# Seven-product weight combinations: sums formed by accumulating transfers on GpSimd's queue instead of subtractions on VectorE

## The chip, the cores and the metric

The kernel runs on one core of one Trainium2 chip. The metric is device time in microseconds (us) of one execution, and the compared figure is the median of several executions. Five engines matter: TensorE (PE, with its weight loads PEld), VectorE (DVE), ScalarE (ACT), GpSimd (POOL) and SyncE (SP), which here only issues transfers. A row of a profile such as "L808 ACT CAST whi<-raw" reads: line 808 of the kernel, on ScalarE, writes tile `whi` from tile `raw`.

## What is computed

Two layers of a decoder trunk on 256 tokens of width 2048, in float32. Nearly all the work is large matrix products of the 256 tokens with weights that are read once from memory.

```python
def hybrid_layer(x, ...):
    h = rms_norm(x, g_mix_pre)
    proj = h @ w_in                       # 2048 x 11776: pool, conv, q, k, v, swish gate, 3 branch gates
    u_pool, u_conv, q, k, v, g_ret, gate_pre = split(proj)
    y_pool = pool_mixer(u_pool, ...) @ w_pool_proj
    y_conv = conv_module(u_conv, ...) @ w_conv_proj
    y_ret = retention(q, k, v, g_ret, ...) @ w_ret_proj
    gates = sigmoid(gate_pre.reshape(B, S, 3, D))
    merged = gates[:, :, 0] * y_pool + gates[:, :, 1] * y_conv + gates[:, :, 2] * y_ret
    x = x + rms_norm(merged @ w_out, g_mix_post)
    h = rms_norm(x, g_ffn_pre)
    a, b = split(h @ w_ffn_in, 2)         # 2048 x 11264
    x = x + rms_norm((silu(a) * b) @ w_ffn_out, g_ffn_post)   # 5632 x 2048
    return x
```

## The kernel before

**Chunks and loads.** Every product is cut into chunks of 512 output columns (`chunks`; a chunk holds the weight, its first row, its depth in blocks of 128 rows, its first column, the name of the left operand, the function that takes the result away, and what must be finished first). Tokens come in two halves of 128, h = 0 and h = 1. A weight comes in loads of two blocks, a tile `raw` of 128 x 2 x 512 float32 (512 KB), issued by SP from a pool of six (`RAWBUFS`). `load()` splits a `raw` in two: ScalarE writes the rounded part `whi` (line 808) and VectorE the rest `wlo` (line 809). Both come from pools of seven (`WBLOCKS`). A product of one block with one half is three matmuls in a PSUM bank (lines 830 to 832: high by high, low by high, high by low).

**Order.** `items` is the planned list of loads. `multiply(0)` walks it for the first half; `multiply(1)` follows four loads behind (`LAG = 8` blocks) for the second half. In all that follows, a **pass** is one load against one half: two blocks, six matmuls. Splits stand as far ahead in the program as the seven buffers let them.

**Seven products.** 44 pairs of neighbouring chunks n, n+1 (`mixed`) save one product in eight on four of their blocks (a quad): rows r, r+1 and rows r+2, r+3, columns of n and of n+1 give a 2 x 2 matrix of weight loads

- b11 (upper rows, chunk n), b12 (upper rows, chunk n+1), b21 (lower rows, chunk n), b22 (lower rows, chunk n+1),

and the two token halves by the two row pairs give a 2 x 2 matrix of left operands a11, a12, a21, a22. Seven products replace eight: four weight combinations t1 to t4 are formed from the b blocks, and sums of the a blocks are formed once per left operand by `token_sums` (lines 187 to 206). Each of the seven is used in one pass only, since a combination belongs to both halves. The other loads of a pair, called P (chunk n) and Q (chunk n+1) below, take two passes each: six of each where the chunk is 16 blocks deep (40 pairs), four of each where it is 12 deep (the 4 pairs of the first part of the second feed-forward product).

The combinations are made in place on the `raw` tiles by VectorE:

```python
        if kind == "t1":
            kept["b12"] = fetch(i, n + 1, k)
            dve.tensor_tensor(kept["b11"], kept["b12"], kept["b11"], op=ALU.subtract)   # line 788
...
        elif kind == "t4":
            dve.tensor_tensor(kept["b21"], kept["b21"], kept["b22"], op=ALU.subtract)   # line 795
...
        if kind == "b22":                                                    # after its own split
            dve.tensor_tensor(kept["b12"], raw, kept["b12"], op=ALU.subtract)           # line 812
            dve.tensor_tensor(raw, raw, kept["b11"], op=ALU.subtract)                   # line 813
```

so a pair of depth 16 runs as P P P P P b11 t1 P b21 b22 Q t2 Q t3 Q t4 Q Q Q. Partial results of the seven are joined by four VectorE operations per pair (lines 868 to 882).

Of the kernel before, what the change touches and what calls it, by code (L numbers as in the profile page):

```python
# [18 lines left out]
P = 128  # L19
# [18 lines left out]
LAG = 8  # L38
WBLOCKS = 7
SLOTS = 24  # L40

# [36 lines left out]
def trunk(ctx: ExitStack, tc: tile.TileContext, x, x_cols, positions, g_mix_post, g_ffn_post, w_in, pool_w,  # L78
# [103 lines left out]
    def pre_norm_quad(h, c, gain, mixed):  # L182
        st["xT", h].append(split(transpose4(x_block(h, c)), gain[:, 4 * c:4 * c + 4]))
        if mixed and c == 3 and h == 1:
            add_sums("sum", "xT", 3)

    def token_sums(lhs, c):

        ts = [st[lhs, h][c] for h in range(2)]
        u = slot([P, 2, 4, P])  # L190
        for h in range(2):
            dve.tensor_tensor(u[:, h], ts[h][:, 0].bitcast(F32), ts[h][:, 1].bitcast(F32), op=ALU.add)
            yield 0.7
        a11, a12, a21, a22 = (u[:, h, 2 * i:2 * i + 2] for h in range(2) for i in range(2))
        s = slot([P, 4, 2, P])
        dve.tensor_tensor(s[:, 0], a21, a22, op=ALU.add)
        dve.tensor_tensor(s[:, 1], s[:, 0], a11, op=ALU.subtract)
        yield 0.9
        dve.tensor_tensor(s[:, 2], a11, a21, op=ALU.subtract)
        dve.tensor_tensor(s[:, 3], a12, s[:, 1], op=ALU.subtract)  # L200
        yield 0.9
        hi, lo = slot([P, 4, 2, P], F32R), slot([P, 4, 2, P], F32R)
        act.copy(hi, s)
        dve.tensor_tensor(lo, s, hi.bitcast(F32), op=ALU.subtract)
        st["S", lhs, c] = (hi, lo)
        yield 1.2
# [112 lines left out]
    def add_job(key, gen, light=False):  # L319
        jobs.append([key, gen, 0, light])  # L320

    def add_sums(key, lhs, c):
        jobs.insert(0, [(key, 0), token_sums(lhs, c), 0, True])

    def step_job(job):
        cost = next(job[1], None)
# [173 lines left out]
    def ev_rot(key, qd):  # L500
        def f(h, ps):
            if h == 0:
                st[key, qd] = slot([P, 4, SEQ])
            if key == "qT" and qd == 0:
                finish({("trig", 0)})
                tr = sm.tile([P, 3, 64], F32, name=nm("tr"), tag="tr", bufs=2)
                r = st["rstd", h]
                dve.tensor_scalar(tr[:, 0, :], trig["cos"][:, h * 64:(h + 1) * 64], r, None, op0=ALU.mult)
                dve.tensor_scalar(tr[:, 1, :], trig["sin"][:, h * 64:(h + 1) * 64], r, None, op0=ALU.mult)
                dve.tensor_scalar(tr[:, 2, :], tr[:, 1, :], -1.0, None, op0=ALU.mult)  # L510
                st["tr", h] = tr
# [12 lines left out]
            dve.tensor_tensor(a, a, b, op=ALU.add)  # L524
            dst = st[key, qd][:, :, h * P:(h + 1) * P]
            defer(2 * D_T, lambda: act.copy(dst, transpose4(a)))
            if key == "kT" and qd == 1 and h == 1:
                add_sums("sum", "xT", 3)
        return f

    def ev_v(qd):
# [26 lines left out]
    def ev_y(b, c):  # L558
        def f(h, ps):
# [10 lines left out]
            if b == 2:  # L570
# [3 lines left out]
                def put():  # L574
                    st["mT", h].append(split(transpose4(m)))
                    if h == 1 and c == 0:
                        add_sums("sum", "mT", 0)

                defer(2 * D_T, put)
        return f  # L580
# [38 lines left out]
    def ev_b(first):  # L619
        def f(h, ps, t=None):  # L620
# [9 lines left out]
            def put():  # L630
                hid.append(split(transpose4(u)))
                if first and h == 1:
                    add_sums("sum", "hid", 0)

            defer(D_T, put)
        return f
# [35 lines left out]
    for l in range(DEPTH):  # L672
        wi = w_in[l]

        def gate(b, c, needs=()):
            add(wi, 0, 16, Q_GATE + b * D + c * NB, "xT", ev_gate(b, c), needs)

        def project(b, c):
            w, name = ((w_pool_proj, "pool"), (w_conv_proj, "conv"), (w_ret_proj, "ret"))[b]
# [10 lines left out]
        for b in range(3):  # L690
            for c in (0, 2):
                mix(*GATE_QUADS[b])
                for cc in (c, c + 1):
                    gate(b, cc, ("sum", "sum2")[:len(GATE_QUADS[b])])
                for cc in (c, c + 1):
                    project(b, cc)
        for c in range(4):
            if c == 0:
                mix(0)
            add(w_out[l], 0, 16, c * NB, "mT", ev_out(l, c), ("sum",))  # L700
        ends.append(len(chunks))
        parts = ((0, 3), (3, 7), (7, 11))
        for p, (b0, b1) in enumerate(parts):
            last = p == len(parts) - 1
            for j in range(b0, b1):
                if j:
                    mix(3)
                add(w_ffn_in[l], 0, 16, j * NB, "xT", ev_a, ("sum",) if j else ())
                add(w_ffn_in[l], 0, 16, HIDDEN + j * NB, "xT", ev_b(j == b0))
            for c in range(4):  # L710
                if c == 0 or c == 2 and not last:
                    mix(0)
                add(w_ffn_out[l], b0 * 4, (b1 - b0) * 4, c * NB, "hid", ev_ffn(l, c, p, last), ("sum",))
        ends.append(len(chunks))

    SEVEN = (("b11", 0), ("t1", 0), ("b21", 2), ("b22", 2), ("t2", 0), ("t3", 0), ("t4", 2))


    paired = {0} | {e for e in ends[:-1]}
# [8 lines left out]
    while n < len(chunks):  # L728
        ks = list(range(0, chunks[n][2], LOAD))
        if n in mixed:  # L730
            ks = [k for k in ks if k // 4 not in mixed[n]]

            head = max(LAG // LOAD, len(ks) - 1) if len(mixed[n]) == 1 else len(ks)
            for k in ks[:head]:
                plan("", n, k)
            for q in mixed[n][:-1]:
                for kind, d in SEVEN:
                    plan(kind, n, 4 * q + d)
            q = 4 * mixed[n][-1]
            plan("b11", n, q)  # L740
            plan("t1", n, q)
            for k in ks[head:]:
                plan("", n, k)
            plan("b21", n, q + 2)
            plan("b22", n, q + 2)
            for k, kind, kq in zip(ks, ("t2", "t3", "t4"), (q, q, q + 2)):
                plan("", n + 1, k)
                plan(kind, n, kq)
            for k in ks[3:]:
                plan("", n + 1, k)  # L750
            side = (n, n + 1)
        else:
            side = (n, n + 1) if n in paired else (n,)
# [4 lines left out]
            final[m] = ks[-1] + LOAD - 1  # L758
        n += len(side)
        count[n] = len(items)  # L760
    raws = {}
    wt = {}
    banks = {}
    loaded = [0]
    done = [0, 0]

    def fetch(i, n=None, k=None):
        if n is None:
            n, k = items[i][1:]
        w, r0, kt, c0 = chunks[n][:4]  # L770
        r = (r0 + k) * P
        raw = wpool.tile([P, LOAD, NB], F32, name=nm("raw"), tag="raw", bufs=RAWBUFS)
        step = LOAD if i else 1
        for kk in range(0, LOAD, step):
            nc.sync.dma_start(raw[:, kk:kk + step], w[r + kk * P:r + (kk + step) * P, c0:c0 + NB]
                              .rearrange("(k p) n -> p k n", p=P))
        raws[i] = raw
        return raw

# [2 lines left out]
    def load():  # L782

        i = loaded[0]
        kind, n, k = items[i]
        if kind == "t1":
            kept["b12"] = fetch(i, n + 1, k)
            dve.tensor_tensor(kept["b11"], kept["b12"], kept["b11"], op=ALU.subtract)  # L788
            raw = kept["b11"]
        elif kind == "t2":  # L790
            raw = kept["b22"]
        elif kind == "t3":
            raw = kept["b12"]
        elif kind == "t4":
            dve.tensor_tensor(kept["b21"], kept["b21"], kept["b22"], op=ALU.subtract)  # L795
            raw = kept["b21"]
        elif kind == "b22":
            raw = kept[kind] = fetch(i, n + 1, k)
        else:
            if i not in raws:  # L800
                fetch(i)
            raw = raws.pop(i)
            kept[kind] = raw
        hi = wpool.tile([P, LOAD, NB], F32R, name=nm("whi"), tag="whi", bufs=WBLOCKS)
        lo = wpool.tile([P, LOAD, NB], F32R, name=nm("wlo"), tag="wlo", bufs=WBLOCKS)
        step = LOAD if i else 1
        for kk in range(0, LOAD, step):
            act.copy(hi[:, kk:kk + step], raw[:, kk:kk + step])  # L808
            dve.tensor_tensor(lo[:, kk:kk + step], raw[:, kk:kk + step], hi[:, kk:kk + step].bitcast(F32),  # L809
                              op=ALU.subtract)  # L810
        if kind == "b22":
            dve.tensor_tensor(kept["b12"], raw, kept["b12"], op=ALU.subtract)  # L812
            dve.tensor_tensor(raw, raw, kept["b11"], op=ALU.subtract)  # L813
        for kk in range(LOAD):
            wt[i + kk] = (hi[:, kk, :], lo[:, kk, :])
        loaded[0] += LOAD
# [18 lines left out]
    def mixed_product(kind, n, k, w):  # L835

        kk, last = k % 2, k % 2 == 1 and k // 4 == mixed[n][-1]
        lhs, outs = chunks[n][4], (chunks[n][5], chunks[n + 1][5])

        def a_part(h):  # L840
# [20 lines left out]
            bank(s_part(0))  # L861
        elif kind == "b22":
            product((0, n + 1), "mm0", s_part(3), w, False)
        elif kind == "t2":
            x = bank(s_part(1))
            if last:
                s = st["sum", 1, n]
                dve.tensor_tensor(s, s, x, op=ALU.add)
                st["sum", 0, n] = t2("dt", 2)
                dve.tensor_tensor(st["sum", 0, n], s, banks["t1", n], op=ALU.add)  # L870
        elif kind == "t3":
            x = bank(s_part(2))
            if last:
                s = st["sum", 1, n]
                dve.tensor_tensor(s, s, x, op=ALU.add)
        elif kind == "t4":
            y = product((1, n), "mm1", a_part(1), w, last)
            if last:
                assert items[done[1]][1:] > (n, final[n])
                s = st["sum", 1, n]  # L880
                outs[0](1, y, s)
                dve.tensor_tensor(s, s, banks["t1", n], op=ALU.add)

    def multiply(h):
        i = done[h]
# [4 lines left out]
                mixed_product(kind, n, k, wt.pop(i))  # L890
        else:
            w, r0, kt, c0, lhs, evac, needs = chunks[n]
            if k == (4 if mixed.get(n, mixed.get(n - 1)) == (0,) else 0):
# [158 lines left out]
```

## Time and profile before

| | |
|---|---|
| three runs, us | 2845.32, 2845.46, 2847.76 (median 2845.46) |
| profiled execution, us | 2846.71, its span on the core 2844.9 |
| TensorE busy | 2825.8 us, 12788 instructions, granted clock 0.999 |
| VectorE busy | 2257.6 us (79%) |
| ScalarE busy | 1434.2 us (50%) |
| GpSimd busy | 104.4 us (4%), no transfers on its queue |
| transfers | 569.78 MB, mean 200 GB/s |

A busy share says how long an engine held an instruction; the chain of waits says which engine ended last at each step. Matmuls overlap: one lasts 0.39 us in the records while a new one starts every 0.23 us, so the time of a matmul is read from the distance of two starts.

### The profile page before, as it was taken

How to read it: one execution, taken by the hardware profiler on the slowest of the kernel's cores; microseconds unless marked ns; L12 is line 12 of the kernel's file. 1: busy time of each engine (PE TensorE's matmuls, PEld its weight loads, DVE VectorE, ACT ScalarE, POOL GpSimd, SP SyncE). 2: the span in 40 equal slices, each digit the busy share in tenths (PEclk: the TensorE clock that was granted, in tenths of full speed). 3: DMA queues.
4: the chain of work that ended last, by engine and by line, in shares of the span. 5: the costliest groups of instructions: out<-in, count | busy, mean ns of one | idle time of the engine just before them, and what ended most of it. 6: DMA issues, size and time to landing. Idle time of an engine off the chain costs nothing.

```text
span 2844.9 us, 34694 instructions
## 1 busy us (share of the span) xinstructions
PE 2825.8 (99%) x12788; PEld 2333.2 (82%) x12788; DVE 2257.6 (79%) x2671; ACT 1434.2 (50%) x1638; POOL 104.4 (4%) x102
## 2 busy tenths in 40 slices
PE   9999999999999999999999999999999999999998
PEld 7888888888888888888888888888888888888887
DVE  6987888776888887787769778787768888887886
ACT  5444544554555554454554455455555554544553
POOL 0000001100100000000000000010000000000000
PEclk9999999999999999999999999999999999999999
DMA  8665655557655665665766655655676565656654
GB/s 306 189 191 172 202 183 188 178 191 259 187 199 200 215 199 172 220 198 192 243 213 186 191 175 177 208 178 180 207 263 189 185 215 188 218 174 201 217 194 166
DMA packets 293898, 569.78 MB, mean 200 GB/s; under 512 B 18272, under 2 KB 21600, under 8 KB 293728
## 3 DMA queue, kind: packets, MB, share of 16 engines
q1 hardware_dynamic: 293728, 567.57, 61.8%
q8 instruction: 100, 1.64, 0.2%
q14 instruction: 70, 0.57, 0.1%
HBM read 559.11 MB, written 8.39 MB: 199 GB/s over the span
## 4 chain that ended last, share of the span: by engine, by line
PE 96%; DVE 3%; ACT 0%; POOL 0%; issue 0%; DMA 0%; SPq 0%; DVEq 0%; POOLq 0%; ACTq 0%
PE mm L832 31%; PE mm L831 31%; PE mm L830 31%; PE tp L143 2%; DVE wlo L809 1%; ACT whi L808 0%; DVE slot L245 0%; PE tp L444 0%; DVE slot L137 0%; DMA raw<-in_w_in 0%; DVE ta L134 0%; DVE ta L464 0%; PE sc L408 0%; PE sc L452 0%; PE sc L434 0%
## 5 line engine op out<-in xcount | busy, mean ns | idle before, releaser
L808 ACT CAST whi<-raw 128x1024 fp32r<-128x1024 f32 (+1 forms) x1157 | 1200.7, 1052 | 1188.3 <-PE mm L831 842.7
L809 DVE TENSOR_TENSOR wlo<-raw,whi 128x1024 fp32r<-128x1024 f32 (+1 forms) x1157 | 1407.7, 1235 | 408.1 <-ACT whi L808 393.1
L830 PE MATMUL mm<-whi,slot 128*128 128x512 f32 x4008 | 1570.4, 392 | 1.2 <-ACT whi L808 0.7
L832 PE MATMUL mm<-wlo,slot 128*128 128x512 f32 x4008 | 1562.5, 390 | 3.6 <-DVE wlo L809 3.5
L831 PE MATMUL mm<-whi,slot 128*128 128x512 f32 x4008 | 1561.4, 390 | 0.7 <-DVE slot L137 0.6
L832 PEld LDWEIGHTS mm<-wlo,slot 128*128 128x128 f32 x4008 | 752.3, 188 | 164.0 <-DVE wlo L809 7.7
L830 PEld LDWEIGHTS mm<-whi,slot 128*128 128x128 f32 x4008 | 752.6, 188 | 155.5 <-ACT whi L808 3.7
L831 PEld LDWEIGHTS mm<-whi,slot 128*128 128x128 f32 x4008 | 752.9, 188 | 154.8 <-DVE slot L137 2.7
L365 DVE SCALAR_TENSOR_TENSOR slot<-slot,par,slot 128x237 f32<-128x237 f32 (+25 forms) x240 | 98.1, 461 | 0.5
L137 DVE TENSOR_TENSOR slot<-tp,slot 128x512 fp32r<-128x512 f32 x60 | 40.8, 685 | 47.4 <-ACT slot L136 47.4
L136 ACT CAST slot<-tp 128x512 fp32r<-128x512 f32 x60 | 35.2, 586 | 84.3 <-PE tp L143 84.3
L569 POOL TENSOR_TENSOR slot<-slot,tb 128x512 f32<-128x512 f32 x32 | 52.9, 1658 | 413.9 <-DVE tb L568 404.7
L237 POOL TENSOR_SCALAR ms_o<-ssq_t 128x1 f32<-128x1 f32 x8 | 1.5, 192 | 1472.8 <-DVE ssq_t L235 1472.8
L788 DVE TENSOR_TENSOR raw<-raw,raw 128x1024 f32<-128x1024 f32 x44 | 53.8, 1223 | 1.3
L813 DVE TENSOR_TENSOR raw<-raw,raw 128x1024 f32<-128x1024 f32 x44 | 53.7, 1221 | 0.9
L812 DVE TENSOR_TENSOR raw<-raw,raw 128x1024 f32<-128x1024 f32 x44 | 53.6, 1218 | 0.3
L795 DVE TENSOR_TENSOR raw<-raw,raw 128x1024 f32<-128x1024 f32 x44 | 53.6, 1218 | 0.2
L625 DVE TENSOR_TENSOR ta<-dt,mm 128x512 f32<-128x512 f32 x40 | 27.3, 683 | 21.5 <-PE mm L832 21.5
L143 PEld LDWEIGHTS tp<-ident,ta 128*128 128x128 f32 x272 | 33.8, 141 | 9.6 <-issue 1.1
L136 ACT CAST slot<-ta 128x512 fp32r<-128x512 f32 x40 | 24.8, 619 | 32.9 <-DVE ta L134 27.6
L143 PE MATMUL tp<-ident,ta 128*128 128x128 f32 x272 | 40.7, 272 | 0.3 <-DVE ta L379 0.2
L148 ACT ACTIVATE tb<-slot 128x512 f32<-128x512 f32 x48 | 30.0, 626 | 21.7 <-DVE slot L648 14.9
(136 smaller groups left out, 948.7 us busy)
## 6 DMA issues: line engine op xcount, KB each, us to landing
raw<-in_w_in SPq DMA_DIRECT2D x367, 512.0 KB, 4.0
raw<-in_w_ffn_in SPq DMA_DIRECT2D x352, 512.0 KB, 4.6
raw<-in_w_ffn_out SPq DMA_DIRECT2D x176, 512.0 KB, 4.7
raw<-in_w_out SPq DMA_DIRECT2D x64, 512.0 KB, 4.4
raw<-in_w_ret_proj SPq DMA_DIRECT2D x32, 512.0 KB, 5.5
raw<-in_w_pool_proj SPq DMA_DIRECT2D x16, 512.0 KB, 5.5
raw<-in_w_conv_proj SPq DMA_DIRECT2D x16, 512.0 KB, 5.7
x<-slot SPq DMA_DIRECT2D x12, 512.0 KB, 4.4
```

The source lines that it names most:

```text
L136: act.copy(t[:, 0], src)
L143: pe.transpose(tp[:, j, :], src[:, j * P:(j + 1) * P], ident)
L365: dve.scalar_tensor_tensor(acc[:, ct, s:], hT[:, ct, :SEQ - s], w[:, TAPS - 1 - s:TAPS - s], acc[:, ct, s:], op0=ALU.mult, op1=ALU.add)
L788: dve.tensor_tensor(kept["b11"], kept["b12"], kept["b11"], op=ALU.subtract)
L795: dve.tensor_tensor(kept["b21"], kept["b21"], kept["b22"], op=ALU.subtract)
L808: act.copy(hi[:, kk:kk + step], raw[:, kk:kk + step])
L809: dve.tensor_tensor(lo[:, kk:kk + step], raw[:, kk:kk + step], hi[:, kk:kk + step].bitcast(F32), op=ALU.subtract)
L812: dve.tensor_tensor(kept["b12"], raw, kept["b12"], op=ALU.subtract)
L813: dve.tensor_tensor(raw, raw, kept["b11"], op=ALU.subtract)
L830: pe.matmul(ps, a[0], w[0], start=first, stop=False)
L831: pe.matmul(ps, a[1], w[0], start=False, stop=False)
L832: pe.matmul(ps, a[0], w[1], start=False, stop=stop)
```

## The change

The signs in the seven products are chosen anew, so that every combination of weights is a sum:

- t1 = b11 + b12, t2 = t1 + b22, t4 = t2 + b21, all in the tile that b11 was loaded to; t3 = b22 + b12, in the tile of b22.

Each step is a transfer issued on GpSimd's queue that reads the other block from memory again and adds it to the tile (`accum_op=ALU.add`), after the tile's earlier content has been split. VectorE's four subtractions per pair are gone; the separate load of b12 is gone; four accumulating transfers per pair are new. The order of the loads becomes P P P P b11 P b22 P t1 b21 t3 Q t2 Q Q t4 Q Q Q (depth 16) and P P P P b11 b22 t1 b21 t3 Q t2 Q Q t4 Q (depth 12). The wait for the token sums moves to the pass of b22.

```diff
@@ token_sums
-        dve.tensor_tensor(s[:, 0], a21, a22, op=ALU.add)
+        dve.tensor_tensor(s[:, 0], a21, a22, op=ALU.subtract)
...
-        dve.tensor_tensor(s[:, 3], a12, s[:, 1], op=ALU.subtract)
+        dve.tensor_tensor(s[:, 3], a12, s[:, 1], op=ALU.add)
@@ planning of a mixed pair
+            head = LAG // LOAD + 1 - len(quads)
             for k in ks[:head]:
                 plan("", n, k)
...
+            seven("b11")
+            for k in ks[head:-1]:
                 plan("", n, k)
...
+            seven("b22")
+            for k in ks[max(head, len(ks) - 1):]:
+                plan("", n, k)
+            seven("t1", "b21", "t3")
+            for i, k in enumerate(ks):
                 plan("", n + 1, k)
...
+                if i == 0:
+                    seven("t2")
+                if i == min(2, len(ks) - 1):
+                    seven("t4")
@@ load()
+    ADDED = {"b11": (1, 0), "t1": (1, 2), "t2": (0, 2), "b22": (1, 0)}
...
-        if kind == "t1":
-            kept["b12"] = fetch(i, n + 1, k)
-            dve.tensor_tensor(kept["b11"], kept["b12"], kept["b11"], op=ALU.subtract)
...
+        if kind in ("t1", "t2", "t3", "t4"):
+            raw = kept[{"t3": "b22"}.get(kind, "b11"), k // 4]
...
-        if kind == "b22":
-            dve.tensor_tensor(kept["b12"], raw, kept["b12"], op=ALU.subtract)
-            dve.tensor_tensor(raw, raw, kept["b11"], op=ALU.subtract)
+        if kind in ADDED:
+            right, down = ADDED[kind]
+            gp.dma_start(raw, block(n + right, k - k % 4 + down), accum_op=ALU.add)
@@ mixed_product
+        if kind == "b22" and not kk:
+            finish({("sum", chunks[n][4], k // 4)})
...
         elif kind == "t2":
             x = bank(s_part(1))
             if last:
                 s = st["sum", 1, n]
                 dve.tensor_tensor(s, s, x, op=ALU.add)
                 st["sum", 0, n] = t2("dt", 2)
-                dve.tensor_tensor(st["sum", 0, n], s, banks["t1", n], op=ALU.add)
+                dve.tensor_tensor(st["sum", 0, n], banks["t1", n], s, op=ALU.subtract)
+                dve.tensor_tensor(s, s, banks["t3", n], op=ALU.add)
```

How the instructions stand, in one pair of the first layer's first feed-forward product (depth 16). ScalarE before; its rows are the splits in their order: b22 from its own `raw`, a Q, t2 (again from b22's tile `raw_1413`), a Q, t3 (from `raw_1398`, where b12 was), a Q, a SiLU for the preceding result, t4 (from b21's tile), a Q.

```order
L808 CAST whi_1414_6813<-raw_1413_6811 128x1024
L808 CAST whi_1417_6833<-raw_1416_6831 128x1024
L808 CAST whi_1421_6853<-raw_1413_6811 128x1024
L808 CAST whi_1424_6859<-raw_1423_6857 128x1024
L808 CAST whi_1426_6863<-raw_1398_6743 128x1024
L808 CAST whi_1432_6898<-raw_1431_6896 128x1024
L616 ACTIVATE sg_1420_6848<-ta_1419_6846,rstd_1241_5996 128x512
L808 CAST whi_1434_6903<-raw_1409_6792 128x1024
L808 CAST whi_1437_6909<-raw_1436_6907 128x1024
```

ScalarE of the changed kernel at the same place: t1 (tile `raw_1383`, that of b11), a transposed block, b21, t3 (tile `raw_1390`, that of b22), a Q, t2 (`raw_1383`), two Q, the SiLU, t4 (`raw_1383`), a Q.

```order
L810 CAST whi_1401_6777<-raw_1383_6688 128x1024
L137 CAST slot_1400_6768<-tp_1399_6763 128x512
L810 CAST whi_1405_6797<-raw_1404_6795 128x1024
L810 CAST whi_1407_6813<-raw_1390_6728 128x1024
L810 CAST whi_1410_6819<-raw_1409_6817 128x1024
L810 CAST whi_1415_6846<-raw_1383_6688 128x1024
L810 CAST whi_1418_6853<-raw_1417_6851 128x1024
L810 CAST whi_1422_6878<-raw_1421_6876 128x1024
L617 ACTIVATE sg_1414_6841<-ta_1413_6839,rstd_1234_5982 128x512
L810 CAST whi_1424_6882<-raw_1383_6688 128x1024
L810 CAST whi_1427_6888<-raw_1426_6886 128x1024
```

Three splits of one tile now follow each other here, with four instructions of ScalarE between the first and the second of them and three between the second and the third; t3 has moved ahead of t2.

GpSimd's queue of the changed kernel, from the end of the norm before the first feed-forward product to the second pair of it (before, the next instruction after these two norms' rows on this queue stood at the end of the layer).

```order
L126 TENSOR_SCALAR rstd_a_1258_6075<-ssq_t_1257_6073 128x1
L128 TENSOR_TENSOR rstd_1259_6077<-rstd_a_1258_6075,nhalf_78 128x1
L816 DMA raw_1305_6334<-in_w_ffn_in 128x2x512
L816 DMA raw_1313_6375<-in_w_ffn_in 128x2x512
L816 DMA raw_1305_6334<-in_w_ffn_in 128x2x512 x2
L816 DMA raw_1383_6688<-in_w_ffn_in 128x2x512
L816 DMA raw_1390_6728<-in_w_ffn_in 128x2x512
L816 DMA raw_1383_6688<-in_w_ffn_in 128x2x512 x2
```

For each pair the queue holds, in this order, the step to t1, the step to t3, the step to t2 and the step to t4, each behind the split of what the tile held.

More of the change, by code (lines that the diff above doesn't have):

```diff
@@ L184, in pre_norm_quad @@
         if mixed and c == 3 and h == 1:
-            add_sums("sum", "xT", 3)
+            add_sums("xT", 3)
     def token_sums(lhs, c):
@@ L320, in add_job, with add_sums @@
         jobs.append([key, gen, 0, light])
-    def add_sums(key, lhs, c):
-        jobs.insert(0, [(key, 0), token_sums(lhs, c), 0, True])
+    def add_sums(lhs, c):
+        jobs.insert(0, [("sum", lhs, c), token_sums(lhs, c), 0, True])
     def step_job(job):
@@ L527, in f @@
             if key == "kT" and qd == 1 and h == 1:
-                add_sums("sum", "xT", 3)
+                add_sums("xT", 3)
         return f
@@ L576, in put @@
                     if h == 1 and c == 0:
-                        add_sums("sum", "mT", 0)
+                        add_sums("mT", 0)
                 defer(2 * D_T, put)
@@ L632, in put @@
                 if first and h == 1:
-                    add_sums("sum", "hid", 0)
+                    add_sums("hid", 0)
             defer(D_T, put)
@@ L673, in trunk, with gate @@
         wi = w_in[l]
-        def gate(b, c, needs=()):
-            add(wi, 0, 16, Q_GATE + b * D + c * NB, "xT", ev_gate(b, c), needs)
+        def gate(b, c):
+            add(wi, 0, 16, Q_GATE + b * D + c * NB, "xT", ev_gate(b, c))
         def project(b, c):
@@ L693, in trunk @@
                 for cc in (c, c + 1):
-                    gate(b, cc, ("sum", "sum2")[:len(GATE_QUADS[b])])
+                    gate(b, cc)
                 for cc in (c, c + 1):
@@ L699, in trunk @@
                 mix(0)
-            add(w_out[l], 0, 16, c * NB, "mT", ev_out(l, c), ("sum",))
+            add(w_out[l], 0, 16, c * NB, "mT", ev_out(l, c))
         ends.append(len(chunks))
@@ L707, in trunk @@
                     mix(3)
-                add(w_ffn_in[l], 0, 16, j * NB, "xT", ev_a, ("sum",) if j else ())
+                add(w_ffn_in[l], 0, 16, j * NB, "xT", ev_a)
                 add(w_ffn_in[l], 0, 16, HIDDEN + j * NB, "xT", ev_b(j == b0))
@@ L712, in trunk @@
                     mix(0)
-                add(w_ffn_out[l], b0 * 4, (b1 - b0) * 4, c * NB, "hid", ev_ffn(l, c, p, last), ("sum",))
+                add(w_ffn_out[l], b0 * 4, (b1 - b0) * 4, c * NB, "hid", ev_ffn(l, c, p, last))
         ends.append(len(chunks))
-    SEVEN = (("b11", 0), ("t1", 0), ("b21", 2), ("b22", 2), ("t2", 0), ("t3", 0), ("t4", 2))
+    ADDED = {"b11": (1, 0), "t1": (1, 2), "t2": (0, 2), "b22": (1, 0)}
     paired = {0} | {e for e in ends[:-1]}
@@ L730, in trunk, with seven @@
         if n in mixed:
-            ks = [k for k in ks if k // 4 not in mixed[n]]
-            head = max(LAG // LOAD, len(ks) - 1) if len(mixed[n]) == 1 else len(ks)
+            quads = mixed[n]
+            ks = [k for k in ks if k // 4 not in quads]
+            def seven(*kinds):
+                for kind in kinds:
+                    for q in quads:
+                        plan(kind, n, 4 * q + (2 if kind in ("b21", "b22", "t4") else 0))
+            head = LAG // LOAD + 1 - len(quads)
             for k in ks[:head]:
                 plan("", n, k)
[L736 to L742, printed above, removed]
-                plan("", n, k)
-            plan("b21", n, q + 2)
-            plan("b22", n, q + 2)
-            for k, kind, kq in zip(ks, ("t2", "t3", "t4"), (q, q, q + 2)):
+            seven("b11")
+            for k in ks[head:-1]:
+                plan("", n, k)
+            seven("b22")
[3 more added lines that the diff above has]
+            for i, k in enumerate(ks):
                 plan("", n + 1, k)
-                plan(kind, n, kq)
-            for k in ks[3:]:
-                plan("", n + 1, k)
+                if i == 0:
+                    seven("t2")
+                if i == min(2, len(ks) - 1):
+                    seven("t4")
             side = (n, n + 1)
@@ L760, in trunk @@
         count[n] = len(items)
+    first = {}
+    for i, (kind, n, k) in enumerate(items):
+        if not kind:
+            first.setdefault(n, i)
     raws = {}
@@ L765, in trunk, with block, fetch @@
     done = [0, 0]
-    def fetch(i, n=None, k=None):
-        if n is None:
-            n, k = items[i][1:]
+    def block(n, k, kk=0, count=LOAD):
         w, r0, kt, c0 = chunks[n][:4]
-        r = (r0 + k) * P
+        r = (r0 + k + kk) * P
+        return w[r:r + count * P, c0:c0 + NB].rearrange("(k p) n -> p k n", p=P)
+    def fetch(i):
+        kind, n, k = items[i]
+        n += kind == "b22"
         raw = wpool.tile([P, LOAD, NB], F32, name=nm("raw"), tag="raw", bufs=RAWBUFS)
@@ L774, in fetch @@
         for kk in range(0, LOAD, step):
-            nc.sync.dma_start(raw[:, kk:kk + step], w[r + kk * P:r + (kk + step) * P, c0:c0 + NB]
-                              .rearrange("(k p) n -> p k n", p=P))
+            nc.sync.dma_start(raw[:, kk:kk + step], block(n, k, kk, step))
         raws[i] = raw
@@ L785, in load @@
         kind, n, k = items[i]
-        if kind == "t1":
-            kept["b12"] = fetch(i, n + 1, k)
[L788 to L798, printed above, removed]
+        if kind in ("t1", "t2", "t3", "t4"):
+            raw = kept[{"t3": "b22"}.get(kind, "b11"), k // 4]
         else:
@@ L802, in load @@
             raw = raws.pop(i)
-            kept[kind] = raw
+            kept[kind, k // 4] = raw
         hi = wpool.tile([P, LOAD, NB], F32R, name=nm("whi"), tag="whi", bufs=WBLOCKS)
@@ L863, in mixed_product @@
             product((0, n + 1), "mm0", s_part(3), w, False)
+        elif kind == "t3":
+            bank(s_part(2))
         elif kind == "t2":
@@ L869, in mixed_product @@
                 st["sum", 0, n] = t2("dt", 2)
-                dve.tensor_tensor(st["sum", 0, n], s, banks["t1", n], op=ALU.add)
[L871 to L875, printed above, removed]
+                dve.tensor_tensor(st["sum", 0, n], banks["t1", n], s, op=ALU.subtract)
+                dve.tensor_tensor(s, s, banks["t3", n], op=ALU.add)
         elif kind == "t4":
@@ L881, in mixed_product @@
                 outs[0](1, y, s)
-                dve.tensor_tensor(s, s, banks["t1", n], op=ALU.add)
+                dve.tensor_tensor(s, banks["t1", n], s, op=ALU.subtract)
     def multiply(h):
@@ L892, in multiply @@
             w, r0, kt, c0, lhs, evac, needs = chunks[n]
-            if k == (4 if mixed.get(n, mixed.get(n - 1)) == (0,) else 0):
+            if i == first[n]:
                 finish({(s, q) for s in needs for q in (0, h)})
```

## Prediction

> **What bounds the kernel now.** I read the busy times and the clock first, then the chain that ended last, then TensorE's waits, then single stretches.
>
> ```profile
> span 2844.9 us, 34694 instructions
> PE 2825.8 (99%) x12788; PEld 2333.2 (82%) x12788; DVE 2257.6 (79%) x2671; ACT 1434.2 (50%) x1638; POOL 104.4 (4%) x102
> PEclk9999999999999999999999999999999999999999
> PE 96%; DVE 3%; ACT 0%; POOL 0%; issue 0%; DMA 0%; SPq 0%; DVEq 0%; POOLq 0%; ACTq 0%
> ```
>
> TensorE is idle for 2844.9 - 2825.8 = 19.1 us, its clock is full, and 96% of the chain is its own. Two starts in an unbroken run give the price of a matmul:
>
> ```profile
> 1002.53 0.39 PE L830 MATMUL mm<-whi,slot 128*128 128x512 f32 x1
> ...
> 1011.38 0.39 PE L830 MATMUL mm<-whi,slot 128*128 128x512 f32 x1
> ```
>
> They are 39 matmuls apart: 8.85 / 39 = 0.227 us, so a pass (six) takes 1.36 us. The change neither removes nor adds a matmul. So what it can win lies inside the 19.1 us, while any new wait of TensorE adds to the time in full. Where the idle time lies, by stretches (columns: stretch, its length, TensorE busy and records, clock, transfers):
>
> ```profile
> 0.00:25.00 25.00, 22.26 (x82) 1.00 0.94 324
> 325.00:400.00 75.00, 72.41 (x357) 1.00 0.55 173
> 550.00:575.00 25.00, 24.09 (x113) 1.00 0.33 98
> 1400.00:1450.00 50.00, 48.29 (x225) 1.00 0.71 220
> 1700.00:1775.00 75.00, 74.31 (x365) 1.00 0.55 176
> 1975.00:2000.00 25.00, 24.08 (x109) 1.00 0.39 115
> 2825.00:2845.00 20.00, 11.14 (x50) 0.85 0.29 105
> ```
>
> The first and the last (2.7 and 8.9 us) are the start and the end of the program, which the change does not touch. Between them lie 2.6 + 0.9 + 1.7 + 0.7 + 0.9 = 6.8 us: about the most that can be won.
>
> **What goes.** VectorE's four subtractions per pair:
>
> ```profile
> L788 DVE TENSOR_TENSOR raw<-raw,raw 128x1024 f32<-128x1024 f32 x44 | 53.8, 1223 | 1.3
> L813 DVE TENSOR_TENSOR raw<-raw,raw 128x1024 f32<-128x1024 f32 x44 | 53.7, 1221 | 0.9
> L812 DVE TENSOR_TENSOR raw<-raw,raw 128x1024 f32<-128x1024 f32 x44 | 53.6, 1218 | 0.3
> L795 DVE TENSOR_TENSOR raw<-raw,raw 128x1024 f32<-128x1024 f32 x44 | 53.6, 1218 | 0.2
> PE mm L832 <- DVE wlo L809: 1.8, 2, 0.9
> ```
>
> That is 214.7 us of an engine that is beside the path nearly everywhere. The last row (TensorE's waits after 400 us) shows the two places where these subtractions do delay it: 0.9 us each, in the stretches at 550 and 1975, where `wlo` comes late because the subtractions and the token sums stand ahead of it. Those 1.8 us go. In the stretches 325 to 400 and 1700 to 1775, where retention shares VectorE with the first pair (3.3 us together), I count half, 1.6; the 1.7 us at 1400 lie at a norm and stay. Gain: 3.4 us, between 0 and 6.8. The four joining operations (L868 to L882) stay four on VectorE. SP loses 44 of its loads. The token sums keep their operations.
>
> **What comes: a round trip between two splits of one tile.** Before, a combination was ready 1.22 us after its inputs. Now t1, t2 and t4 each need: the split of what the tile holds, GpSimd's issue, the transfer, the next split. TensorE needs them in program order, so each has a fixed number of passes to hide in. ScalarE's splits are held by the seven buffers, not by the loads:
>
> ```profile
> ACT whi L808 <- PE mm L831: 842.7, 608, 4.4
> 1003.97 1.05 ACT L808 CAST whi<-raw 128x1024 fp32r<-128x1024 f32 x1
> 1005.05 1.22 DVE L809 TENSOR_TENSOR wlo<-raw,whi 128x1024 fp32r<-128x1024 f32 x1 [0.20 <-ACT whi L808]
> ```
>
> A split thus starts when the load seven places earlier has had its last pass, and takes 1005.05 + 1.22 - 1003.97 = 2.30 us to the end of `wlo`.
>
> Take the pair of depth 16. t2 stands seven places behind the fifth P; its split can start when that P's second-half pass ends, which runs interleaved with the pass of b21. From there to the pass of t4, TensorE has: t3 (one pass), the first Q with the sixth P's second half (two), t2, Q, Q: six passes, 8.16 us. Into that must go the split of t2 (2.30), the round trip L, and the split of t4 (2.30, less 0.45 since `wlo` is first read by the third matmul), with 0.1 for the signals. That leaves L = 8.16 - 2.30 - 1.85 - 0.1 = 3.9 us. **If the accumulating transfer takes longer than 3.9 us from the end of `wlo` to its landing, TensorE stands still for the rest, once per pair.** Behind the late split of t4 on ScalarE's queue wait the splits of the last three Q; each needs TensorE later, so they shift with it and cost nothing of their own. GpSimd's own waits cost nothing in the feed-forward stages, where its queue has no other work.
>
> The other round trips have more room: b11 to t1 eight passes less a split, 10.9 - 2.4 = 8.5 us; t1 to t2 seven passes, 9.5 - 2.4 = 7.1 us; b22 to t3 as b11. In the four pairs of depth 12 the room between t2 and t4 is five passes: 6.8 - 4.25 = 2.5 us. There b11, b22 and t1 stand side by side, and the three round trips from b11 to t4 follow each other in seventeen passes, 23.1 us: with four splits, 9.2 - 0.45, they leave 14.3 us, so that the wait is the larger of L - 2.5 and 3 L - 14.3.
>
> **The size of L.** No row of before has a transfer on GpSimd's queue. The nearest are the plain loads of the same 512 KB (first row: all feed-forward loads, median to landing; second: all loads into `raw`, least, median and most, 800 to 2000 us):
>
> ```profile
> raw<-in_w_ffn_in SPq DMA_DIRECT2D x352, 512.0 KB, 4.6
> DMA to landing us min/median/max: 3.4/4.5/7.1
> q1 hardware_dynamic: 293728, 567.57, 61.8%
> L125 POOL TENSOR_SCALAR rstd_a<-ssq_t 128x1 f32<-128x1 f32 x8 | 11.9, 1485 | 82.4 <-DVE ssq_t L210 82.3
> ```
>
> Low end: 3.4 us, the fastest plain load, with the addition and the issue at nothing. Above it, an addition must also read the tile that it adds to, a third stream beside one read and one write. The queue row prices a plain load's streams: 0.618 x 2844.9 us for 567.57 MB is 1.62 us per 512 KB (524288 bytes) on all sixteen engines. High end: the median twice over, 9.0 us. GpSimd's issue is software of unknown length; its small operations go up to 1.5 us (L125). I take 4.5 + 1.6 = 6.1 us, nearest to the median load plus one more set of streams, with the issue counted as SP's is, inside the 4.5.
>
> A rule speaks against this wait. The Trainium skill, "DMA: Bandwidth & Descriptors", section "Anatomy of one DMA — SWDGE (gpsimd) path", gives 2.0 us + bytes / 436e3 for a transfer on this path; by it 512 KB would take an estimated 3.2 us, under 3.9, and the change would cost nothing. The trace's plain loads of that size do not come under 3.4 and have a median of 4.5, so here I go by the rows.
>
> **The sum.** 40 pairs x (6.1 - 3.9) = 88.0 us; 4 pairs x (18.3 - 14.3) = 16.0; less 3.4: +100.6 on the span, 2945.5. The profiled execution took 2846.71 - 2844.9 = 1.8 us more than its span, and 1.25 us more than the median shown (2845.46). Against the median: 2845.46 + 100.6 = 2946. With L at 3.4 the sum is 4 x 0.9 = 3.6 less 3.4, no change: 2846. With L at 9.0, t2 is late as well by 9.0 - 7.1: 40 x (5.1 + 1.9) + 4 x 12.7 - 3.4 = +327, 3173.
>
> **Rivals.**
>
> A. The addition is hidden: L is 4.1 us or less, or the room is wider than I count. For it: a plain load can land in 3.4 us, and transfers fill under two thirds of the engines. Against: the median of plain loads is already 4.5, and these transfers carry more. The time is 2846 less 0 to 6.8, near 2843. By the page just named it is this case that happens. This one ends on the other side: it holds from L = 3.9 downwards. Even so a gain over 0.2% (5.7 us; 0.2% is about what a measurement of this kernel can tell from no change) needs nearly all of the 6.8 us. Chance 0.18, mostly "same".
>
> B. L over 7.1 us: software issue of a microsecond or more, additions at half the rate of copies, and loads of SP in the way. Then t2 is late too, and the wait grows twice as fast: at L = 8.0, 40 x (4.1 + 0.9) + 4 x 9.7 - 3.4 = +235, 3081. For it: loads that meet others take up to 7.1 us as they are. Against: the median is far below. Chance 0.22. A clock that falls would come on top. In before, TensorE's longest wait after the start is 1.6 us, and the granted clock stays full:
>
> ```profile
> 382.27 0.63 PE L143 MATMUL tp<-ident,tb 128*128 128x128 f32 x4 [1.56 <-DVE tb L467]
> 380.00:385.00 5.00, 3.44 (x18) 2.50 (x17) 5.00 (x9) 1.57 (x2) 0.00 (x0) 1.00 0.26 95
> ```
>
> The Trainium skill, "TensorE: Matmul & The Clock Gate", section "Part 1: The HAM clock gate (the "warmup" mystery)", says that the clock halves after an idle window of about 3.4 us and needs about as long to come back; by it an estimated 1.7 us more per pair would be lost, 75 us in all, once waits reach that length. No run here shows such a wait.
>
> C. The 132 additional transfers (176 new, 44 gone) make the loads late everywhere. Against: 132 x 3.2 us of streams is 422 us, 15% of the span on top of 61.8%; and ScalarE waits for buffers, not for loads. It would show as waits for plain loads; I give it 0.02, at some 2990.
>
> **Chances and range.** My forecast, a wait at t4 with L between 4.1 and 7.1: 0.58, from 2856 (40 x 0.2 + 4 x 1.6 less 3.4 is +11) to 2998 (40 x 3.2 + 4 x 7.0 less 3.4 is +153); time 2946 at L = 6.1. The range must take in most of A and the nearer half of B, so it runs from 2841 to 3060 (the latter at L about 7.8), leaving out some 0.13. Faster by over 0.2% is 0.04 (the best of A), within 0.2% 0.14 (the rest of A), slower 0.82.
>
> **What the profile of the changed kernel would show.** Right: TensorE idle some 100 us more, in the waits as TensorE or its weight loads waiting for the split of t4 (`whi`, `wlo`), once per pair, some 2 us each, and ScalarE waiting for the transfer on GpSimd's queue; matmul distance 0.227 us as before; VectorE busy near 2043 us; the transfers of line 816 landing in about 6 us; the 0.9 us at 550 and 1975 gone. Wrong: landings under 4 us and TensorE's idle time at 19 us or below (A); waits in front of t2 too, landings over 7 us, or a granted clock below 1.00 in the middle of the run (B). What would upset the whole sum is an error in the room of 3.9 us, which rests on the order of passes and on the seven buffers, not on a row that shows the room itself.

## The result and the profile after

The changed kernel takes 3072.81 us (median of four runs, 3070.3 to 3077.77) against 2846.1 us for the kernel before: a ratio of 1.0798, 95% interval 1.0779 to 1.0817. The forecast was 2946 us in a range from 2841 to 3060. The sign and the place were right; the size was more than twice what I forecast (227 us more, where 100 were forecast), and the time lies outside the range.

The page of the changed kernel, the rows that answer to those of before:

```profile
span 3068.5 us, 35006 instructions
PE 2908.8 (95%) x12788; PEld 2365.9 (77%) x12788; DVE 2066.1 (67%) x2495; ACT 1425.3 (46%) x1638; POOL 311.4 (10%) x278
q1 hardware_dynamic: 281760, 544.50, 52.8%
q0 software_dynamic: 47872, 92.29, 18.4%
L816 POOL DMA_DIRECT2D raw<-in_w_ffn_in x80 | 96.3, 1204 | 823.2 <-DVE wlo L811 778.1
raw<-in_w_ffn_in POOLq DMA_DIRECT2D x80, 512.0 KB, 6.9
raw<-in_w_in POOLq DMA_DIRECT2D x48, 512.0 KB, 7.3
raw<-in_w_ffn_out POOLq DMA_DIRECT2D x40, 512.0 KB, 7.8
```

Two parts make up the 223.6 us by which the span grew. TensorE's idle time is 3068.5 - 2908.8 = 159.7 us instead of 19.1: 140.6 us more. And its busy time grew by 83.0 us, with the same 12788 instructions. The mean granted clock is 0.976 instead of 0.999; by it TensorE ran 2 x 0.024 x 3068.5 = 147 us at half speed. Against the clock before, this loses 0.023 x 3068.5 = 71 us. The other 12 us of busy time are probably no work: a matmul's record lasts 0.39 us, the next could start after 0.227, and where the run breaks these 0.16 us count as busy; 88 such breaks (two in each of 44 pairs) make an estimated 14 us. Where the idle time is, by TensorE's own waits (total, times, longest):

```profile
PE mm L833 <- ACT whi L810: 103.2, 44, 6.3
PE mm L835 <- DVE wlo L811: 20.9, 44, 0.6
PE tp L445 <- DVE ta L380: 9.3, 1, 9.3
```

The two rows together are 124.1 us. Taken one by one, 40 of the first row's waits are for t4, in 40 of the 44 pairs (97.9 us), and so are 37 of the second row's (18.0 us); two of the first row (3.9 us) are for t2 in pairs of depth 12, and two are at the start of the program. The single wait of 9.3 us is a block's transposition in the second layer's retention: VectorE stood behind a `wlo` that waited for a transfer, so the same lateness met another instruction first.

One pair in the first layer's first feed-forward product, in order of time. GpSimd's queue (start, length of the issue), ScalarE's splits, then TensorE's rows around t4, and the clock in single microseconds (stretch, its length, TensorE busy and records, clock, transfers):

```profile
1057.03 1.20 POOL L816 DMA_DIRECT2D raw<-in_w_ffn_in  x1 [25.12 <-DVE wlo L811]
1062.97 1.20 POOL L816 DMA_DIRECT2D raw<-in_w_ffn_in  x1 [4.74 <-DMA raw<-in_w_ffn_in]
1065.92 1.20 POOL L816 DMA_DIRECT2D raw<-in_w_ffn_in  x1 [1.74 <-DVE wlo L811]
1076.57 1.20 POOL L816 DMA_DIRECT2D raw<-in_w_ffn_in  x1 [9.45 <-DVE wlo L811]
...
1069.27 2.00 ACT L810 CAST whi<-raw 128x1024 fp32r<-128x1024 f32 x2 [2.47 <-DMA raw<-in_w_ffn_in]
1073.63 2.95 ACT L810 CAST whi<-raw 128x1024 fp32r<-128x1024 f32 x3 [2.36 <-DMA raw<-in_w_ffn_in]
1084.12 3.89 ACT L810 CAST whi<-raw 128x1024 fp32r<-128x1024 f32 x4 [5.69 <-DMA raw<-in_w_ffn_in]
```

```profile
1083.23 0.39 PE L835 MATMUL mm<-wlo,slot 128*128 128x512 f32 x1
1085.22 0.50 PE L833 MATMUL mm<-whi,slot 128*128 128x512 f32 x1 [1.60 <-ACT whi L810]
1085.56 0.40 PE L834 MATMUL mm<-whi,slot 128*128 128x512 f32 x1
1086.48 0.77 PE L835 MATMUL mm<-wlo,slot 128*128 128x512 f32 x1 [0.52 <-DVE wlo L811]
1087.05 0.63 PE L833 MATMUL mm<-whi,slot 128*128 128x512 f32 x1
1087.47 0.63 PE L834 MATMUL mm<-whi,slot 128*128 128x512 f32 x1
```

```profile
1085.00:1086.00 1.00, 0.73 (x2) 1.00 0.00 0
1086.00:1087.00 1.00, 0.52 (x1) 0.77 0.00 0
1087.00:1088.00 1.00, 1.00 (x4) 0.50 0.47 88
1088.00:1089.00 1.00, 1.00 (x4) 0.50 1.00 346
1089.00:1090.00 1.00, 1.00 (x3) 0.53 0.88 262
1090.00:1091.00 1.00, 1.00 (x6) 1.00 0.93 320
```

The four issues are the steps to t1, t3, t2 and t4. t2's split begins at 1073.63 after a wait for its transfer; its step to t4 is issued at 1076.57; t4's split begins at 1084.12. The issues at 1065.92 and 1076.57 land after:

```profile
DMA to landing us min/median/max: 7.6/7.6/7.6
DMA to landing us min/median/max: 7.5/7.5/7.5
```

TensorE could have begun t4 at 1083.23 + 0.23 = 1083.46 and begins at 1085.22, with the matmul that reads `wlo` another 0.8 us late. Then 3.4 us pass at half the clock: the starts at 1087.05 and 1087.47 are 0.42 us apart instead of 0.227.

### The profile page after: what moved, and what is told of

Read it like the earlier page. It is cut to its first block, busy times and chain, and to the rows that moved or that the text cites. A ratio compares the mean times of both kernels' runs of the same rounds, so it can differ in the third digit from the quotient of the medians.

```text
span 3068.5 us, 35006 instructions
## 1 busy us (share of the span) xinstructions
PE 2908.8 (95%) x12788; PEld 2365.9 (77%) x12788; DVE 2066.1 (67%) x2495; ACT 1425.3 (46%) x1638; POOL 311.4 (10%) x278
## 5 line engine op out<-in xcount | busy, mean ns | idle before, releaser
L810 ACT CAST whi<-raw 128x1024 fp32r<-128x1024 f32 (+1 forms) x1157 | 1185.3, 1050 | 1356.3 <-PE mm L834 752.8
L833 PE MATMUL mm<-whi,slot 128*128 128x512 f32 x4008 | 1598.3, 399 | 109.3 <-ACT whi L810 103.2
L835 PE MATMUL mm<-wlo,slot 128*128 128x512 f32 x4008 | 1589.7, 397 | 21.4 <-DVE wlo L811 20.9
L834 PE MATMUL mm<-whi,slot 128*128 128x512 f32 x4008 | 1583.1, 395 | 4.6 <-DVE slot L138 4.5
L833 PEld LDWEIGHTS mm<-whi,slot 128*128 128x128 f32 x4008 | 766.2, 191 | 283.6 <-ACT whi L810 124.0
L835 PEld LDWEIGHTS mm<-wlo,slot 128*128 128x128 f32 x4008 | 765.1, 191 | 207.9 <-DVE wlo L811 48.4
L834 PEld LDWEIGHTS mm<-whi,slot 128*128 128x128 f32 x4008 | 766.0, 191 | 163.7 <-DVE slot L138 7.9
L816 POOL DMA_DIRECT2D raw<-in_w_ffn_in x80 | 96.3, 1204 | 823.2 <-DVE wlo L811 778.1
L816 POOL DMA_DIRECT2D raw<-in_w_in x48 | 58.2, 1214 | 726.1 <-DMA raw<-in_w_in 447.1
L366 DVE SCALAR_TENSOR_TENSOR slot<-slot,par,slot 128x237 f32<-128x237 f32 (+25 forms) x240 | 97.9, 458 | 0.5
L816 POOL DMA_DIRECT2D raw<-in_w_ffn_out x40 | 48.2, 1205 | 424.1 <-DVE wlo L811 398.4
L617 ACT ACTIVATE sg<-ta,rstd 128x512 f32<-128x512 f32 x40 | 29.0, 726 | 58.0 <-DVE ta L614 58.0
L555 ACT ACTIVATE sg<-sg,rstd 128x512 f32<-128x512 f32 x48 | 34.8, 724 | 40.4 <-DVE sg L553 40.4
L149 ACT ACTIVATE tb<-slot 128x512 f32<-128x512 f32 x48 | 30.1, 628 | 28.3 <-DVE slot L649 21.6
```

Of the source, the lines that this page charges most:

```text
L366: dve.scalar_tensor_tensor(acc[:, ct, s:], hT[:, ct, :SEQ - s], w[:, TAPS - 1 - s:TAPS - s], acc[:, ct, s:], op0=ALU.mult, op1=ALU.add)
L555: act.activation(s, ps, ACT.Sigmoid, scale=st["rstd", h])
L816: gp.dma_start(raw, block(n + right, k - k % 4 + down), accum_op=ALU.add)
L833: pe.matmul(ps, a[0], w[0], start=first, stop=False)
L834: pe.matmul(ps, a[1], w[0], start=False, stop=False)
L835: pe.matmul(ps, a[0], w[1], start=False, stop=stop)
```

## The experiments

In each, "idle" is the span less TensorE's busy time. Ratios are to the kernel before on the same chip.

| kernel | time, us | ratio (95%) | idle | clock |
|---|---|---|---|---|
| before | 2846.1 to 2846.7 | 1 | 19.1 | 0.999 |
| changed | 3072.81 | 1.0798 (1.0779 to 1.0817) | 159.7 | 0.976 |
| order alone, sums on VectorE | 2839.94 | 0.9977 (0.9968 to 0.9987) | 15.3 | 0.999 |
| t4 two loads later | 2939.52 | 1.0318 (1.0301 to 1.0335) | 80.9 | 0.994 |
| copies instead of additions | 2860.78 | 1.0050 (1.0034 to 1.0066) | 27.1 | 0.997 |
| nine idle matmuls before t4 | 3070.75 | 1.0789 (1.0767 to 1.0811) | 100.7 | 0.984 |
| t4's sum alone on VectorE | 2869.95 | 1.0081 (1.0065 to 1.0098) | 32.0 | 0.997 |
| half the bytes per addition | 2851.79 | 1.0019 (1.0009 to 1.0030) | 19.7 | 0.999 |
| four idle matmuls before t4 | 3063.15 | 1.0761 (1.0740 to 1.0783) | 128.1 | 0.981 |
| t2 one load later, t4 after the last Q | 2887.54 | 1.0145 (1.0124 to 1.0165) | 43.1 | 0.993 |

### The order and the signs without the transfers

```diff
+        if kind == "t1":
+            kept["b12", q] = fetch(i, n + 1, k)
+            dve.tensor_tensor(kept["b11", q], kept["b11", q], kept["b12", q], op=ALU.add)
+            dve.tensor_tensor(kept["b12", q], kept["b12", q], kept["b22", q], op=ALU.add)
...
-        if kind in ADDED:
-            right, down = ADDED[kind]
-            gp.dma_start(raw, block(n + right, k - k % 4 + down), accum_op=ALU.add)
+        if kind in ("t1", "t2"):
+            dve.tensor_tensor(raw, raw, kept["b22" if kind == "t1" else "b21", q], op=ALU.add)
```

> The new signs and the new order of loads, with the sums formed by VectorE again: b12 is loaded by SP once more, and four additions of 1.22 us per pair stand where four accumulating transfers were; GpSimd's queue issues none. Theory (the accumulating transfers land too late for t4, and the waits let TensorE's clock fall): the 223.6 us of longer span go, 2843 us, between 2838 and 2850, clock 0.999, TensorE idle 12 to 20 us. Rival 'order' (the order itself, or the moved wait for the token sums, costs the time): 2950 us or more, idle time at t4 as with the transfers.

Measured: 2839.94 us. Its page has these rows (all four additions are on lines 803, 804 and 822):

```profile
span 2837.7 us, 34729 instructions
PE 2822.4 (99%) x12788; PEld 2333.8 (82%) x12788; DVE 2266.2 (80%) x2671; ACT 1433.5 (51%) x1638; POOL 109.3 (4%) x102
L822 DVE TENSOR_TENSOR raw<-raw,raw 128x1024 f32<-128x1024 f32 x88 | 107.4, 1220 | 1.7
```

All of the loss is gone, and with VectorE as busy as before. So neither the order, nor the signs, nor the moved wait for the token sums costs anything. The new order, with its signs, is worth some 6.5 us, and this version beats both kernels. Of the 7.2 us by which its span is shorter, 3.8 are idle time of TensorE and 3.4 are busy time, so it is not simply the 6.8 us of idle time between start and end that the prediction offered as the most.

### Where the additions are paid: bytes, not the queue

```diff
-            gp.dma_start(raw, block(n + right, k - k % 4 + down), accum_op=ALU.add)
+            gp.dma_start(raw, block(n + right, k - k % 4 + down))
```

> The transfers on GpSimd's queue copy instead of adding (the additions of weight blocks are left out; everything else, waits and bytes read from memory included, stays). Theory as in the prediction (a transfer that adds carries a third stream, 1.6 us): landing 1 to 2 us sooner, 6 to 6.5 us instead of 7.5, two of them in a row, so 2 to 4 us per pair: 2850 to 2900 us. Rival 'software queue' (the time is in GpSimd's issue and in the queueing behind plain loads, not in the addition): landing as before within 0.5 us, 3040 to 3075 us.

Measured: 2860.78 us. Its rows for GpSimd's queue:

```profile
q0 software_dynamic: 25344, 92.29, 10.7%
L816 POOL DMA_DIRECT2D raw<-in_w_ffn_in x80 | 57.9, 724 | 784.5 <-DVE wlo L811 781.0
raw<-in_w_ffn_in POOLq DMA_DIRECT2D x80, 512.0 KB, 4.2
```

A copy from the same queue, with the same bytes from memory and the same waits, lands after 4.2 us where the addition took 6.9, and it leaves only 14 us of the 227. The queue rows give the engines' time for each: 0.184 x 3068.5 / 176 = 3.21 us per addition, 0.107 x 2860.0 / 176 = 1.74 us per copy, and 1.62 us per load by SP in the kernel before. GpSimd's issue is 1.20 us for an addition and 0.72 for a copy. So of the 2.7 us between the landings, 1.5 would be the engines' and 0.5 the issue; the other 0.7 I did not separate (the engines being busy longer also means more meeting of other loads).

Half the size of each addition:

```diff
-            gp.dma_start(raw, block(n + right, k - k % 4 + down), accum_op=ALU.add)
+            gp.dma_start(raw[:, :1], block(n + right, k - k % 4 + down, 0, 1), accum_op=ALU.add)
```

> Each accumulating transfer carries one of its two blocks (256 KB instead of 512; the second block of every combination is left unsummed). Theory (the landing is paid by bytes: 3.2 us of the sixteen engines for 512 KB of addition against 1.6 for a copy, and the issue of 1.2 us by descriptors): landing near 5 us instead of 6.9 to 7.8, 2 us less twice per pair, 2845 to 2890 us. Rival 'fixed latency': landing stays over 6.5 us and the time over 2990 us.

Measured: 2851.79 us. The profiled execution took 2847.25 us, with TensorE idle for 19.7 us and these rows:

```profile
L816 POOL DMA_DIRECT2D raw<-in_w_ffn_in x80 | 69.3, 866 | 768.1 <-DVE wlo L811 765.3
raw<-in_w_ffn_in POOLq DMA_DIRECT2D x80, 256.0 KB, 4.3
```

256 KB less take 2.6 us less. There is no large fixed price on this queue: a straight line through the two sizes would leave 1.7 us. 176 accumulating transfers that land after 4.3 us leave the time within 0.3% of before, 12 us over the version with the sums on VectorE, which has the same order. So their number and their waits on GpSimd cost little by themselves.

### Room instead of speed

t4 two loads later, and then t2 one load later and t4 after the last load of the chunk:

```diff
-                if i == min(2, len(ks) - 1):
+                if i == min(4, len(ks) - 1):
```

> Only t4 moves: it stands two loads of the second chunk later (after the fifth Q of six; in the pairs of depth 12 after the last Q). Theory: the round trip from t2 to t4 gains at least two passes, 2.7 us, and up to 5.4 with the second-half passes between; the wait of some 2.8 us per pair shrinks to under 1 us, and without waits of that length the clock stays full: 2848 to 2880 us. Rival 'traffic' (the 132 additional transfers make everything late): 3000 us or more, since no transfer goes. Rival 'order': as before, about 3070.

Measured: 2939.52 us. Some 133 of the 227 us of the loss are gone, but 2848 to 2880 was expected. TensorE's waits:

```profile
PE mm L833 <- ACT whi L810: 27.4, 19, 3.6
PE mm L835 <- DVE wlo L811: 18.4, 32, 1.1
PE tp L144 <- DVE ta L628: 8.8, 8, 1.6
```

The 40 waits for t4 in the first row have become 14 (21.6 us; three of the 19 are for t2, two are at the start of the program), and the third row is new.

```diff
-                if i == 0:
+                if i == 1:
                     seven("t2")
-                if i == min(2, len(ks) - 1):
+                if i == len(ks) - 1:
                     seven("t4")
```

> t2 stands one load of the second chunk later (after its second Q) and t4 after its last Q. Theory (room between the steps): both round trips gain at least a pass (1.4 us), the second up to three more than in the changed kernel; with t4 alone two Q later the time was 2939 us, most of the rest in the second feed-forward product; now 2850 to 2900 us. Rival (what stays is not room but plain loads that wait for the tile of b11, which is held still longer): 2930 us or more.

Measured: 2887.54 us. TensorE's first row of waits is now

```profile
PE mm L833 <- ACT whi L810: 17.5, 7, 4.7
```

Room for both steps brings back 185 of 227 us, with every one of the 176 additions still there. What stays lies for the most part in the four pairs of depth 12: from one pair's copy of the b11 product (L860) to the next, the stretches that hold them take 40.0, 37.3, 41.3 and 38.4 us against 31.8, 34.0, 31.8 and 34.0 before. Four of the seven waits, 15.2 us, are for t4 in these pairs. There the edit moves t2 and t4 by one load each, so that two loads of the second chunk stand between them, as in the changed kernel: the second round trip got no more room, while it got that of two loads more in the pairs of depth 16. The run before, with t4 alone moved, has three loads there, and in it these four pairs wait for t4 for 9.6 us, against 17.5 in the changed kernel.

### The last step alone

```diff
-        if kind in ADDED:
+        if kind == "t2":
+            dve.tensor_tensor(raw, raw, kept["b21", k // 4], op=ALU.add)
+        elif kind in ADDED:
```

> Only the last of the four steps is changed: t4 = t2 + b21 is formed by VectorE (1.22 us, b21 is in SBUF anyway), while t1, t3 and t2 stay accumulating transfers on GpSimd's queue (132 instead of 176). Theory (transfers cost only where their round trip has no room; the two in a row from t1 to t4 have none): the waits at t4 go, the clock stays at 0.99 or above, 2842 to 2870 us; the pairs of depth 12 may keep a wait at t2. Rival 'any transfer on this queue costs' (in proportion): three quarters of the 227 us stay, about 3015 us.

Measured: 2869.95 us, at the upper end of what was expected. One of four transfers fewer removes 203 of the 227 us, so a proportional price per transfer is excluded. What stays is 30 us over the version with all sums on VectorE. The row of its largest wait, 5.2 us over nine times, shows that nothing recurs once per pair any more:

```profile
PE mm L837 <- DVE wlo L811: 5.2, 9, 0.7
```

### The clock

Matmuls of no use in a fresh bank ahead of t4, nine and then four (`recent` is the left operand and the weights of the preceding Q):

```diff
         elif kind == "t4":
+            if not kk:
+                f = psum.tile([P, NB], F32, name=nm("fill"), tag="sc", bufs=4)
+                for _ in range(9):
+                    pe.matmul(f, recent[0], recent[1], start=True, stop=True)
```

> Nine matmuls of no use (one fresh PSUM bank, operands of the preceding Q) stand ahead of each t4, 9 x 0.227 = 2.0 us of the wait of some 2.6. Theory 'clock' (after each wait TensorE runs at half speed for some 3.4 us, which is the 83 us by which its busy time grew): the clock is back at 0.99 or above, and the time falls by 50 to 83 us in spite of the added work: 2990 to 3020 us. Rival (busy time grew by slower operand reads beside the added transfers, not by the clock): no gain, 3073 us or up to 90 us (44 x 2.0) more.

> Four matmuls of no use ahead of each t4 instead of nine: 0.9 us, which fits into nearly every wait. Nine matmuls left the time at 3070.8 us, but where a pair's wait was long they brought the clock back (half-speed time 98 us instead of 145). Theory 'clock' (waits of over some 2 us make the clock fall for stretches of 3.4 us): the added work costs nothing, idle stretches get under the limit in most pairs, half-speed time falls from 145 to under 60 us, which is 40 us or more: 3000 to 3035 us. Rival: the clock falls whatever fills the wait: 3070 us or, with the 44 x 0.9 us of work in the way, up to 3110.

Measured: 3070.75 and 3063.15 us. Both totals miss what I expected. With nine, the added 44 x 9 x 0.227 = 90 us of work took only 59 us out of the idle time. In the gate stage (the first six stretches of each layer from one pair's L861 copy to the next) the nine made the time 6 and 7 us longer than in the changed kernel, in the eight stretches of the second feed-forward product 3 us. The bank that they take is one of four that the seven products and retention use as well: in the run with four, TensorE waits 7.9 us ahead of it, in two places, for an operation of VectorE that joins partial results. As a cure it fails. As a measurement it is clean in sixteen stretches of the first feed-forward product (both layers, second and third part; from the copy of a pair's b11 product, L860 or L861, to that of the next), where t4 is the only thing that TensorE waits for. One of them in the changed kernel and with nine:

```profile
1062.84:1110.27 47.43, 45.30 (x196) 0.96 0.76 211
```

```profile
1066.94:1112.46 45.52, 45.44 (x205) 1.00 0.80 220
1087.57 2.20 PE L884 MATMUL fill<-whi,slot 128*128 128x512 f32 x9
1089.61 0.39 PE L834 MATMUL mm<-whi,slot 128*128 128x512 f32 x1
```

With 2.0 us of work more the stretch is 1.9 us shorter, at full clock throughout. Over the sixteen: 744.5 us in the changed kernel, with 34.0 idle and 30.7 at half speed (nine falls of 3.4 us); 732.6 with nine matmuls, 7.3 idle and none at half speed; 732.5 with four, 16.2 idle and 13.7 at half speed (four falls). There, the fall of the clock is a consequence of the waits, and half of the half-speed time is lost time.

## Why the prediction was wrong

**The place and the mechanism were right.** TensorE waits for t4, in 40 of the 44 pairs, because two accumulating transfers follow each other on one tile. VectorE is busy for 2066 us, where 2043 was forecast: its records are 215 us less in sum, but busy time counts overlapping records once. What this relief is worth, no run shows. The gain of 3.4 us was put down to it, yet the waits at 550 and 1975 are gone as well in the version that has the new order and all four sums on VectorE, so they went with the order.

**The room of 3.9 us was the step that failed first.** I let t2's split begin when the load seven places earlier had had its last pass, six passes ahead of t4. The rows above contradict it: six passes before 1083.46 is 1075.30, and t2's split began at 1073.63, after waiting 2.36 us for its data. So its buffer came free at least 1.7 us earlier than by that rule. That a combination, which needs one pass only, had given its `whi` back early is what I take for the reason; no row shows it. ScalarE's wait ended with the landing, so t2 was held by its own transfer, and the room must be counted over both steps. From the issue of the step to t2 (1065.92) to the latest start of t4's split without a wait (1083.46 + 0.45 - 2.30 = 1081.61), less t2's split with its handover (1076.57 - 1073.63 = 2.94), 12.75 us remain for two landings: 6.4 each. With L = 6.1 that is enough: with the room counted rightly, my L would have forecast no wait in this pair. The room was too small and L too small, and the two errors worked against each other. That 100.6 us were forecast where the idle time grew by 140.6 is in part luck.

**L was mis-sized: 6.1 us taken, 6.9 to 8.3 measured** as medians by weight. By step, read from the 176 single landings: 6.0 on average for the step to t1, 6.4 for t3, 8.1 for t2 and 7.8 for t4. The additional streams were right (1.5 us more of the engines than a copy, 1.6 taken). The issue, which I counted as SP's, is 1.2 us instead of 0.37, and the two late steps land later than the two early ones; so do the copies (4.3, 4.3, 5.0 and 5.4 us on average), and why is not shown. In the pair above 7.6 and 7.5 us, plus 0.07 from each landing to its split, are 15.2 against 12.75: 2.5 us too late, and TensorE's wait is 1.76 + 0.8.

**The clock was left out of the sum.** It stands in rival B as something on top, once waits reach 3.4 us. This is the largest part of what the sum missed: of 223.6 - 100.6 = 123 us some 71 are the clock, 40 are waiting, and 12 are the rest of TensorE's longer busy time. Without the clock's part the span would have grown by some 153 us, and the time would lie inside the range. The Trainium skill's page "TensorE: Matmul & The Clock Gate" says, in "Part 1: The HAM clock gate (the "warmup" mystery)", that the clock stays at half speed until TensorE has been busy for a window of about 3.4 us, and the trace agrees: the clock's shortfall in the rows above, 0.23 + 0.5 + 0.5 + 0.47 = 1.70 us, is that of 3.4 us at half speed. But I took its idle window as a limit for a single wait, and the trace does not bear that out: here 1.8 us of standing still and 0.8 soon after were enough.

**Rival B came nearest** (3081 at L = 8.0), but by luck: its sum has 235 us of waiting and no clock, where the idle time grew by 140.6 us, and TensorE waits for t2's `whi` in two pairs only. Rival A is excluded by the landings. Rival C is excluded by the copies, whose number and whose bytes from memory are the same and cost 14 us, and by the version with t2 and t4 later, where all 176 additions stay and 41 us of the 227 are left.

What stays open: whether waits for t4 in the pairs of depth 12 can be ended by room alone (more room between t2 and t4 shortens them there too, but no run ended them), why a fall of the clock follows one wait and not another, and which part of the order gives its 6.5 us.

## What to carry to other kernels

When an in-order engine at full use must read a tile that is rewritten several times, count the whole chain from the first rewrite to the last use, not the last gap: a 1.2 us operation on an engine with slack can be cheaper than a transfer that takes none of that engine's time. Price a transfer that adds at about twice a copy in the transfer engines' time (here 3.21 against 1.74 us) and with a longer issue, and give it room before it is needed. A wait of two microseconds on TensorE can cost nearly four (with one fall of the clock, 1.7 us of loss, on top), so a change that puts one wait in each block should be priced with the clock in the sum.

## What the runs showed of the hardware that I had not expected

- 512 KB added on GpSimd's queue kept the sixteen transfer engines for 3.21 us, a copy on the same queue for 1.74 us; the issue took 1.20 against 0.72 us of GpSimd, and 0.87 for 256 KB added.
- The clock falls after quite short waits, and not after every one: in the sixteen stretches, stretches with 1.6 and 2.1 us of idle time in all had one fall of 3.4 us each, and one with 3.4 us had none.
- Useless matmuls in the place of a wait shortened those stretches from 744.5 to 732.6 us in sum, though they added 32.6 us of work.
